# Hybrid RWKV-7 / gated-delta layer on one core: two column blocks of the first projection share one PSUM bank and are taken out by one operation

## The chip, the cores and the metric

The kernel runs on one core of a Trainium2 chip. The metric is device time in microseconds (us). The kernel before takes 1256.82 us as the median of three runs (1255.65 to 1258.12). The profile is one further execution of the same program: 1255.44 us, of which 1253.70 us lie between its first and its last instruction (its span).

The engines are called as in the profile: PE does matmuls (PEld is its weight load), DVE is the vector engine, ACT the scalar engine, POOL the general one, and SP issues most DMAs. Each engine works through its own instructions strictly in the order in which they were laid down when the program was built.

## The reference

One layer with 2048 channels over 256 positions, batch 1, all in float32:

```python
h = rms_norm(x, attn_norm_w)
proj = h @ w_in                                   # 2048 x 6448
y_a = rwkv7_mixer(proj[..., :3360], ...)          # token shift, then a recurrence over 256 steps, 16 heads of 64
y_b = gdn_mixer(proj[..., 3360:], ...)            # conv of width 4 and silu on q, k, v; gated delta rule; gate silu(z)
x = x + concatenate([y_a, y_b]) @ w_out
h = rms_norm(x, ffn_norm_w)
x = x + (silu(h @ w_gate) * (h @ w_up)) @ w_down  # 5632 wide
return rms_norm(x, final_norm_w)
```

Token shift is `p + (prev - p) * mu`, with `prev` the position before. The convolution of the second mixer reads the three positions before as well.

## The kernel before

**Projection.** Positions lie along the free dimension, channels on the 128 partitions. Both operands of every large matmul are split into a high and a low part (`split`, L244): ACT writes the rounded high part `wh`, DVE subtracts it from the source and writes the low part `wl`. One weight tile is 128x1024, loaded by one DMA of SP into `raw` (three buffers), split into `wh` and `wl` (two buffers each) and used by 24 matmuls of 256 columns: 16 of the high part (L220 and L223, in turn) and 8 of the low part (L220). A column block of the first projection has 128 output channels and takes two such tiles, so 48 matmuls, into the first 256 columns of one PSUM bank (tag `pb`, two banks in turn). These projection matmuls are called fillers below, since everything else on PE stands between them.

**Evacuation.** After each block DVE multiplies the bank by `rstd` into an SBUF tile `pr` with four zero columns ahead of it (`evac_norm`, L232; two tiles in turn). Then either the token shift follows (ACT L238, DVE L239), or the convolution (`conv_silu`: ACT L667, three DVE operations at L669), or, for z, nothing but a silu. There are 24 blocks of k, r and v for the first mixer, 16 of q, k and v for the second, and 8 of z. Three blocks at the very start (`ps_first`) go their own way.

**The side work.** The two mixers run beside the projection as generators (`prep`, `chain`, `gdn_v`, `gdn`), which go on as soon as their inputs exist. Each ends in recurrences over four chunks. Ahead of a recurrence stands the inverse of triangular blocks (`tri_inverse`, L336): 62 small DVE operations (L352, L354), a trip through DRAM (`sX`, L360, L363), then two sets of small matmuls (`psF`, `psO`). There are three inverses, one after another in the same buffers: r0 and r1 (first mixer, two halves of its heads) and g (second mixer).

**The second mixer's end.** In its last chunk `psOg` (L938) is scaled by ACT (L942), completed by DVE (L944, eight heads), squared and summed by ACT (L949), turned into a reciprocal root by small DVE operations (L951 and `rsqrt`), applied by ACT (L954), and transposed by PE (`ps_og`, L964). DVE multiplies that with z (L967), and the result is split into `ys`.

**The output projection** (L1015) runs over two halves of its inner dimension: first all 16 blocks with the first mixer's output (16 tiles, 384 fillers), then all 16 with the second mixer's. The second pass can't begin before `ys` of the second mixer is there, and no other work for PE stands between the passes. The feed-forward part follows.

**The order.** Loads, splits and evacuations run at high priority. Which instruction stands where on each engine is laid down by a scheduler that plays the program through when it is built; the side work fills the gaps that it sees. A change of a few instructions can so move others far away.

Of the kernel before, what the change touches and what calls it, by code (L numbers as in the profile page):

```python
# [9 lines left out]
F32 = mybir.dt.float32  # L10
# [3 lines left out]
AF = mybir.ActivationFunctionType  # L14
ALU = mybir.AluOpType
AX = mybir.AxisListType

P = 128
T = 256
# [13 lines left out]
VEC = {}  # L33
# [8 lines left out]
OMU = VEC["om"] - VEC["mu_k"]  # L42
# [7 lines left out]
def trunk_kernel(ctx, tc, xT, vecs, fnw, w_up, a_up, g_up, w_in, w_ab, w_out, w_gu, w_dn, out):  # L50
    nc = tc.nc
    V, S, G, PE, SY = nc.vector, nc.scalar, nc.gpsimd, nc.tensor, nc.sync

    cp_ = ctx.enter_context(tc.tile_pool(name="consts", bufs=1))
    wp = ctx.enter_context(tc.tile_pool(name="weights", bufs=1))
    act = ctx.enter_context(tc.tile_pool(name="act", bufs=4))
    pm = ctx.enter_context(tc.tile_pool(name="pm", bufs=2, space=bass.MemoryType.PSUM))
    dr = ctx.enter_context(tc.tile_pool(name="dr", bufs=1, space=bass.MemoryType.DRAM))

    def hi():  # L60
        return tc.high_priority(offset=HI)
# [11 lines left out]
    def mps(name, tag="mr"):  # L73
        return pm.tile([P, 512], F32, tag=tag, name=name)


    vec = cp_.tile([P, NVEC], F32, name="vec")
# [3 lines left out]
    def vc(name, i=0, rows=slice(0, P)):  # L81
        c = VEC[name] + i
        return vec[rows, c:c + 1]
# [34 lines left out]
    rstd = cp_.tile([P, T], F32, name="rstd")  # L118

    with hi():  # L120
        V.memset(rstd, 0.0)
        ps = mps("ps_warm")
# [6 lines left out]
    GS = cp_.tile([P, T], F32, name="GS")  # L129
    GT = cp_.tile([P, 2, 104], F32, name="GT")  # L130
    egc = cp_.tile([P, 8, NCH], F32, name="egc")
    prs = [cp_.tile([P, 260], F32, name=f"pr{i}") for i in range(2)]
    for pr in prs:
        G.memset(pr[:, 0:4], 0.0)

    def rsqrt(y, xh, tag):

# [27 lines left out]
    def tick():  # L165
        for g in list(side):
            while not g.done and g.step():
                pass
# [8 lines left out]
    def load_split(src, by_k=False, whole=False):  # L177

        with hi():
            if first:  # L180
                raw = first.pop(0)
            else:
                raw = wp.tile([P, 1024], F32, tag="raw", name="raw", bufs=RAW)
                SY.dma_start(out=raw.rearrange("p (c f) -> p c f", c=4) if by_k else raw, in_=src)
            wh = wp.tile([P, 1024], F32R, tag="wh", name="wh", bufs=WH)
            wl = wp.tile([P, 1024], F32R, tag="wl", name="wl", bufs=WL)
            both = [(wh[:, h * 512:h * 512 + 512], wl[:, h * 512:h * 512 + 512]) for h in range(2)]
            if whole:
                split(wh, wl, raw)
                return both  # L190
            it = iter(both)
            return halves_of(raw, lambda: next(it), by_k)

    def halves_of(raw, places, by_k=False):
        parts = []
        r4 = raw.rearrange("p (c k f) -> p k c f", c=4, k=2)
        for h in range(2):
            wh, wl = places()
            src, oh, ol = raw[:, h * 512:h * 512 + 512], wh, wl
            if by_k:  # L200
                src, oh, ol = r4[:, h], wh.rearrange("p (c f) -> p c f", c=4), wl.rearrange("p (c f) -> p c f", c=4)
            S.activation(oh, src, AF.Copy)  # L202
            V.tensor_tensor(ol, src, oh, ALU.subtract)  # L203
            parts.append((wh, wl))
        return parts

    def proj(parts, tag="pb"):

        ps = pm.tile([P, 512], F32, tag=tag, name="psb")
        for j, (src, rhs) in enumerate(parts):  # L210
            products(ps, load_split(src, whole=True), rhs, j == 0, j == len(parts) - 1)
        return ps

    def products(ps, parts, rhs, first, last, by_k=False):

        order = [(k, low) for low in range(2) for k in range(8)]
        for k, low in sorted(order) if by_k else order:
            w = parts[k // 4][low][:, k % 4 * P:k % 4 * P + P]
            rt, ri = rhs[k]
            PE.matmul(ps[:, 0:T], w, rt[:, ri, 0:T], start=(first and k == 0 and not low),  # L220
                      stop=(last and k == 7 and low == 1))
            if not low:
                PE.matmul(ps[:, 0:T], w, rt[:, ri, T:], start=False, stop=False)  # L223
            tick()

    prn = [0]

    def evac_norm(ps):

        prn[0] += 1  # L230
        pr = prs[prn[0] % 2]
        V.tensor_tensor(pr[:, 4:260], ps[:, 0:T], rstd, ALU.mult)  # L232
        return pr

    def evac_shift(ps, mu, out):
        with hi():
            pr = evac_norm(ps)
            S.activation(out, pr[:, 4:260], AF.Copy, scale=vec[:, mu + OMU:mu + OMU + 1])  # L238
            shifted[0] = V.scalar_tensor_tensor(out, pr[:, 3:259], vec[:, mu:mu + 1], out, ALU.mult, ALU.add)  # L239
        return pr  # L240

    shifted = [None]

    def split(hi_ap, lo_ap, src, scale=None):  # L244
        if scale is None:
            S.activation(hi_ap, src, AF.Copy)  # L246
            V.tensor_tensor(lo_ap, src, hi_ap, ALU.subtract)  # L247
        else:
            S.activation(hi_ap, src, AF.Copy, scale=scale)
            V.scalar_tensor_tensor(lo_ap, src, scale, hi_ap, ALU.mult, ALU.subtract)  # L250
# [31 lines left out]
    ps_first = [mps("psb", tg) for tg in ("mc", "mg", "mc")]  # L282
    for q in range(2):
        for i in range(3):
            if not xs:
                split_x(0)
            parts = load_split(w_first[i][q])
            if len(xs) < 4:
                split_x(len(xs))
            products(ps_first[i], parts, [(xs[2 * q + k // 4], k % 4) for k in range(8)], q == 0, q == 1, True)  # L290
# [3 lines left out]
    ps = mps("ps_ss")  # L294
# [11 lines left out]

    xk = [(xs[k // 4], k % 4) for k in range(KB)]

    def proj_in(cb):
        return proj([(w_in[cb, q], xk[8 * q:8 * q + 8]) for q in range(2)])  # L310


    def sigmoid(o, x):
        S.activation(o, x, AF.Tanh, scale=0.5)
# [1 line left out]

    pl = rp.tile([P, 2, T], F32, tag="kt", name="pl", bufs=2)
    for i in range(2):
        evac_shift(ps_first[i], VEC["mu_l"] + i, pl[:, i, :])
    S.activation(twa[0:64, :], pl[0:64, 0, :], AF.Tanh)  # L320
    V.tensor_copy(twa[64:128, :], pl[64:128, 0, :])
    sigmoid(sgd1, pl[:, 1, :])
    pl2 = rp.tile([P, T], F32, tag="al1", name="pl2")
    pr = evac_shift(ps_first[2], VEC["mu_l"] + 2, pl2)
    sigmoid(sgd2[0:32, :], pl2[0:32, :])
    ra, rb = slice(32, 40), slice(64, 72)
# [322 lines left out]
    def rwkv_stream(hf):  # L649
        for gr in range(2):  # L650
            for i, (d, mu, tag, nb) in enumerate(((kt, "mu_k", "kt", 2), (rt, "mu_r", "rt", 2), (vt, "mu_v", "vt", 4))):
                f = hf * 4 + gr * 2
                t = rp.tile([P, 2, T], F32, tag=tag, name=f"{tag}{hf}{gr}", bufs=nb)
                for m in range(2):
                    evac_shift(proj_in(2 + ((hf * 2 + gr) * 3 + i) * 2 + m), VEC[mu] + f + m, t[:, m, :])
                vready[(hf, gr)] = shifted[0]
                d[(hf, gr)] = t


    def conv_silu(ti, b0, outt):  # L660
        for m in range(2):
            ps = proj_in(2 * ti + m)
            tb = outt[:, m, :]
            with hi():
                pr = evac_norm(ps)
                c0 = (b0 + m) * 4
                S.activation(tb, pr[:, 4:260], AF.Copy, scale=vc("conv", c0 + 3))  # L667
                for i in range(3):
                    V.scalar_tensor_tensor(tb, pr[:, 1 + i:257 + i], vc("conv", c0 + i), tb, ALU.mult, ALU.add)  # L669
        with hi():  # L670
            return S.activation(outt, outt, AF.Silu)
# [304 lines left out]
    Side(gdn_v())  # L976
    Side(gdn())
    rwkv_stream(0)
    rwkv_stream(1)
    gdn_stream()  # L980

    for i in range(4):
        z = rp.tile([P, 2, T], F32, tag=("kt", "rt")[i % 2], name="zs", bufs=2)
        if i == 3:

            last2 = [pm.tile([P, 512], F32, tag="pb", name="psb") for _ in range(2)]
            for q in range(2):
                for m in range(2):
                    products(last2[m], load_split(w_in[48 + m, q], whole=True), xk[8 * q:8 * q + 8], q == 0, q == 1)
        for m in range(2):  # L990
            ps = last2[m] if i == 3 else proj_in(42 + 2 * i + m)
            with hi():
                V.tensor_tensor(z[:, m, :], ps[:, 0:T], rstd, ALU.mult)
                if m:
                    S.activation(z, z, AF.Silu)
        zs[i] = z
    drain()
    yg = gout[-1]
# [5 lines left out]
    for src in (yR[0], yR[1], yg[:, 0:4, :], yg[:, 4:8, :]):  # L1004
        t = act.tile([P, 4, 2 * T], F32R, tag="act", name="ys")
# [9 lines left out]
    for q in range(2):  # L1015
        for kb in range(KB):
            ps = proj([(w_out[kb, q], yk[8 * q:8 * q + 8])])
# [4 lines left out]
            if kb % 4 == 0:  # L1022
                pool, tag = ((rp, "ar1"), (rp, "bkn1"), (rp, "UV1"), (act, "act"))[kb // 4]
# [11 lines left out]
    ps = mps("ps_ss2")  # L1035
# [152 lines left out]
    for tb in range(2):  # L1188
        pieces = [(0, 512), (512, 512), (1024, 512)] + [[(1536, 512)], [(1536, 256), (1792, 256)]][tb]
        for j, (c0, w) in enumerate(pieces):  # L1190
            ps = mps("psd", ("mr", "mc", "mg")[nbank[0] % 3])[:, 0:w]
# [101 lines left out]
```

## Time and profile before

| | us |
|---|---|
| median of three runs | 1256.82 |
| the profiled execution | 1255.44 |
| its span | 1253.70 |
| PE busy (8134 matmuls) | 1234.8 (98%) |
| DVE busy (1635 operations) | 834.3 (67%) |
| ACT busy (1199 operations) | 651.3 (52%) |
| mean granted TensorE clock | 0.995 |

Busy time of PE is not all work: matmuls are pipelined, a 256-column one is shown as some 0.28 us long though the next starts 0.12 us after it. So short waits vanish in that row, and long ones show as idle time. The first projection and the side work fill the span up to about 398 us, the first pass of the output projection goes to about 458 us, the second to about 510 us, and the feed-forward part takes the rest. DVE is busiest in the first 350 us.

### The profile page before, as it was taken

The page shows a single profiled execution, that of the slowest core. Times are in us where ns is not written, and L with a number is a line of the kernel's source. Part 1 is how long each engine was busy: PE and PEld are TensorE (multiplying, and loading weights), DVE is VectorE, ACT ScalarE, POOL GpSimd, SP SyncE. Part 2 cuts the span into 40 slices and gives each one's busy share as a digit, 9 for nine tenths or more (in the row PEclk, how much of TensorE's full clock was granted, in tenths as well). Part 3 has the DMA queues.
Part 4 walks back from the last instruction along what each step waited for, and adds up shares of the span by engine and source line. Part 5 has one row for each costly group of instructions (what it writes and reads, how often), then busy time and mean ns, then how long its engine had stood idle before and what let it go on. Part 6 is the DMA issues. An engine that isn't in the chain of part 4 may idle for free.

```text
span 1253.7 us, 21133 instructions
## 1 busy us (share of the span) xinstructions
PE 1234.8 (98%) x8134; PEld 1087.0 (87%) x8134; DVE 834.3 (67%) x1635; ACT 651.3 (52%) x1199; POOL 17.8 (1%) x63
## 2 busy tenths in 40 slices
PE   8999999999999999999999999999999999999997
PEld 8999999999999989888888888888888888878886
DVE  7987887977966877565555555555656565665554
ACT  7575665667546456554444444444444444454443
POOL 3000000000000000000000000000000000000000
PEclk9999999999999999999999999999999999999999
DMA  7455665575573445676666666666676666676641
GB/s 248 153 169 179 169 170 149 169 186 139 196 213 118 145 159 186 172 205 194 190 190 197 188 193 192 194 190 196 187 198 182 189 190 195 203 236 193 193 151 67
DMA packets 175702, 226.68 MB, mean 181 GB/s; under 512 B 52273, under 2 KB 144561, under 8 KB 175345
## 3 DMA queue, kind: packets, MB, share of 16 engines
q1 hardware_dynamic: 170896, 221.54, 60.4%
q10 hardware_dynamic: 4560, 2.74, 0.8%
q8 instruction: 64, 1.05, 0.4%
q0 software_dynamic: 144, 1.05, 0.2%
q14 instruction: 38, 0.30, 0.1%
HBM read 218.75 MB, written 4.46 MB: 178 GB/s over the span
## 4 chain that ended last, share of the span: by engine, by line
PE 88%; DVE 5%; DMA 3%; issue 1%; ACT 1%; SPq 0%; ACTq 0%; DVEq 0%
PE psq L1070 37%; PE psd L1147 17%; PE psb L220 16%; PE psb L223 8%; DVE wl L247 2%; PE psT L1102 1%; DMA sX_r<-X_r 1%; DMA raw_end<-in_w_dn 1%; DMA st_r<-sX_r 1%; PE ps_A L485 1%; PE psd L1198 1%; PE psd L1196 1%; PE psd L1197 1%; DMA A_g<-sG 0%; PE psSg L923 0%
## 5 line engine op out<-in xcount | busy, mean ns | idle before, releaser
L203 DVE TENSOR_TENSOR wl<-raw,wh 128x512 fp32r<-128x512 f32 x524 | 340.7, 692 | 273.5 <-ACT wh L202 271.8
L202 ACT ACTIVATE wh<-raw 128x512 fp32r<-128x512 f32 x524 | 302.5, 626 | 363.9 <-PE psq L1070 192.4
L1070 PE MATMUL psq<-wh,x2s 128*128 128x512 f32 x1408 | 377.4, 390 | 0.8 <-ACT wh L202 0.8
L1070 PEld LDWEIGHTS psq<-wh,x2s 128*128 128x128 f32 x1408 | 263.7, 188 | 56.2 <-ACT wh L202 1.7
L1070 PE MATMUL psq<-wl,x2s 128*128 128x512 f32 x704 | 217.2, 389 | 0.0
L220 PE MATMUL psb<-xs,wh 128*128 128x256 f32 x816 | 206.4, 287 | 2.4 <-ACT wh L202 1.7
L223 PE MATMUL psb<-xs,wh 128*128 128x256 f32 x816 | 206.0, 286 | 0.0
L1147 PE MATMUL psd<-wh,h 128*128 128x512 f32 x640 | 203.2, 391 | 1.0 <-ACT wh L202 1.0
L246 ACT ACTIVATE wh<-raw 128x1024 fp32r<-128x1024 f32 x128 | 135.4, 1058 | 87.4 <-PE psb L223 67.8
L247 DVE TENSOR_TENSOR wl<-raw,wh 128x1024 fp32r<-128x1024 f32 x128 | 156.1, 1220 | 11.1 <-ACT wh L246 10.9
L220 PEld LDWEIGHTS psb<-xs,wh 128*128 128x128 f32 x816 | 156.8, 192 | 4.4 <-ACT wh L202 2.4
L223 PEld LDWEIGHTS psb<-xs,wh 128*128 128x128 f32 x816 | 156.8, 192 | 1.2 <-issue 0.7
L1070 PEld LDWEIGHTS psq<-wl,x2s 128*128 128x128 f32 x704 | 132.0, 188 | 27.6
L1147 PEld LDWEIGHTS psd<-wh,h 128*128 128x128 f32 x640 | 119.2, 188 | 25.8 <-ACT wh L202 1.7
L220 PE MATMUL psb<-xs,wl 128*128 128x256 f32 x816 | 127.1, 287 | 0.9 <-DVE wl L247 0.7
L1147 PE MATMUL psd<-wl,h 128*128 128x512 f32 x320 | 124.6, 389 | 0.0
L220 PEld LDWEIGHTS psb<-xs,wl 128*128 128x128 f32 x816 | 109.8, 192 | 2.8 <-DVE wl L247 1.1
L1147 PEld LDWEIGHTS psd<-wl,h 128*128 128x128 f32 x320 | 60.1, 188 | 12.7
L223 PE MATMUL psb<-ys,wh 128*128 128x256 f32 x256 | 64.6, 288 | 2.5 <-DVE ys L247 2.5
L220 PE MATMUL psb<-ys,wh 128*128 128x256 f32 x256 | 64.8, 289 | 0.2 <-ACT ys L246 0.2
L223 PEld LDWEIGHTS psb<-ys,wh 128*128 128x128 f32 x256 | 50.1, 196 | 2.8 <-DVE ys L247 2.7
L1155 DVE TENSOR_TENSOR acc<-acc,psd 128x512 f32<-128x512 f32 x80 | 49.5, 682 | 1.8 <-PE psd L1147 1.8
(315 smaller groups left out, 1026.8 us busy)
## 6 DMA issues: line engine op xcount, KB each, us to landing
raw<-in_w_gu SPq DMA_DIRECT2D x176, 512.0 KB, 4.9
raw<-in_w_in SPq DMA_DIRECT2D x99, 512.0 KB, 3.5
raw<-in_w_dn SPq DMA_DIRECT2D x80, 512.0 KB, 4.3
raw<-in_w_out SPq DMA_DIRECT2D x32, 512.0 KB, 3.5
raw_end<-in_w_dn SPq DMA_DIRECT2D x8, 512.0 KB, 4.2
xraw<-in_xT SPq DMA_DIRECT2D x8, 256.0 KB, 5.8
x<-in_xT SPq DMA_DIRECT2D x1, 2048.0 KB, 9.7
raw<-in_w_ab SPq DMA_DIRECT2D x2, 512.0 KB, 4.9
```

The lines of the kernel that those rows point to most:

```text
L202: S.activation(oh, src, AF.Copy)
L203: V.tensor_tensor(ol, src, oh, ALU.subtract)
L220: PE.matmul(ps[:, 0:T], w, rt[:, ri, 0:T], start=(first and k == 0 and not low), stop=(last and k == 7 and low == 1))
L223: PE.matmul(ps[:, 0:T], w, rt[:, ri, T:], start=False, stop=False)
L246: S.activation(hi_ap, src, AF.Copy)
L247: V.tensor_tensor(lo_ap, src, hi_ap, ALU.subtract)
L485: PE.matmul(psA[h][:, ch, :], bk[hr, ch].rearrange("p a t -> p (a t)"), ar[hr, p, ch].rearrange("p a t -> p (a t)"), start=True, stop=True)
L1070: last = PE.matmul(banks[tb], t[:, ri, o + tb * P:o + tb * P + P], w, start=(k == 0 and o == 0 and w is wh), stop=(k == KB - 1 and w is wl))
L1102: ms.append(PE.transpose(ps[b][:, o:o + P], sg[tb][:, (2 * b + i) * P:(2 * b + i) * P + P], ident))
L1147: m = PE.matmul(banks[tb * 2 + cg], st, parts[cg][w], start=(i == 0 and w == 0 and st is hh), stop=(i == n - 1 and st is hl))
L1155: V.tensor_tensor(acc[:, tb, cs], acc[:, tb, cs], banks[tb * 2 + cg], ALU.add)
L1196: PE.matmul(ps, hh, wh, start=(i == 0), stop=False)
```

## The change

Two neighbouring column blocks now go to the two halves of one bank, and one DVE operation takes both out. `proj_in2` runs the blocks one after the other, tiles in the same sequence as before. `prs` is one tile with two halves, in place of two tiles in turn. The shift and the convolution still work on one block at a time, but both blocks of a pair now follow the pair's evacuation. Of the 46 blocks that went through `proj_in`, 23 pairs are made; the three first blocks and the last two of z keep an evacuation each.

```diff
-    prs = [cp_.tile([P, 260], F32, name=f"pr{i}") for i in range(2)]
-    for pr in prs:
-        G.memset(pr[:, 0:4], 0.0)
+    prs = cp_.tile([P, 2, 260], F32, name="prs")
+    G.memset(prs[:, :, 0:4], 0.0)
...
+    def proj_in2(cb):
+        ps = pm.tile([P, 512], F32, tag="pb", name="psb")
+        for m in range(2):
+            for q in range(2):
+                products(ps[:, m * T:m * T + T], load_split(w_in[cb + m, q], whole=True), xk[8 * q:8 * q + 8],
+                         q == 0, q == 1)
+        return ps
...
     def evac_norm(ps):
-        prn[0] += 1
-        pr = prs[prn[0] % 2]
-        V.tensor_tensor(pr[:, 4:260], ps[:, 0:T], rstd, ALU.mult)
-        return pr
+        V.tensor_tensor(prs[:, :, 4:260], ps.rearrange("p (m t) -> p m t", m=2), rstd[:, None, :].to_broadcast([P, 2, T]),
+                        ALU.mult)
+
+    def shift(pr, mu, out):
+        S.activation(out, pr[:, 4:260], AF.Copy, scale=vec[:, mu + OMU:mu + OMU + 1])
+        shifted[0] = V.scalar_tensor_tensor(out, pr[:, 3:259], vec[:, mu:mu + 1], out, ALU.mult, ALU.add)
...
-                for m in range(2):
-                    evac_shift(proj_in(2 + ((hf * 2 + gr) * 3 + i) * 2 + m), VEC[mu] + f + m, t[:, m, :])
+                ps = proj_in2(2 + ((hf * 2 + gr) * 3 + i) * 2)
+                with hi():
+                    evac_norm(ps)
+                    for m in range(2):
+                        shift(prs[:, m], VEC[mu] + f + m, t[:, m, :])
...
     def conv_silu(ti, b0, outt):
-        for m in range(2):
-            ps = proj_in(2 * ti + m)
-            tb = outt[:, m, :]
-            with hi():
-                pr = evac_norm(ps)
+        ps = proj_in2(2 * ti)
+        with hi():
+            evac_norm(ps)
+            for m in range(2):
+                tb, pr = outt[:, m, :], prs[:, m]
...
+        if i < 3:
+            ps = proj_in2(42 + 2 * i)
             with hi():
-                V.tensor_tensor(z[:, m, :], ps[:, 0:T], rstd, ALU.mult)
-                if m:
-                    S.activation(z, z, AF.Silu)
+                V.tensor_tensor(z, ps.rearrange("p (m t) -> p m t", m=2), rstd[:, None, :].to_broadcast([P, 2, T]),
+                                ALU.mult)
```

The program built from it stands in another order at many places. Three are shown.

**DVE, the first pair of k** (`kt`; `pr_123`, `pr_124` and `prs` are the evacuated blocks; the small rows belong to the gates of the second mixer). Before, from the shift of the pair's first block to that of its second:

```order
L239 SCALAR_TENSOR_TENSOR kt_457<-pr_123,vec,kt_457 128x256
L678 TENSOR_SCALAR g_e<-gu 8x256
L247 TENSOR_TENSOR wl<-raw,wh 128x1024
L232 TENSOR_TENSOR pr_124<-psb,rstd 128x256
L315 TENSOR_SCALAR sgd_116<-sgd_116 32x256
L679 TENSOR_TENSOR g_e<-g_e,gu 8x256
L247 TENSOR_TENSOR wl<-raw,wh 128x1024
L689 TENSOR_SCALAR gu<-gu 8x256
L239 SCALAR_TENSOR_TENSOR kt_457<-pr_124,vec,kt_457 128x256
```

The same place after the change:

```order
L236 TENSOR_TENSOR prs<-psb,rstd 128x2x256
L255 TENSOR_TENSOR wl<-raw,wh 128x1024
L687 TENSOR_TENSOR g_e<-g_e,gu 8x256
L320 TENSOR_SCALAR sgd_116<-sgd_116 32x256
L241 SCALAR_TENSOR_TENSOR kt_455<-prs,vec,kt_455 128x256 x2
```

Two evacuations of 256 columns have become one of 2x256, and both shifts stand behind it, with the split of a weight tile between.

**SP, the DRAM trip of inverse g** (`sX_g` is the DRAM copy of the inverse, `st_g` and `TTg` are read from it; `raw<-in_w_in` is a weight tile of the first projection, `raw<-in_w_out` one of the output projection). Before:

```order
L360 DMA sX_g<-X_g 1024x1x32 x2
L184 DMA raw<-in_w_in 128x1024
L363 DMA st_g<-sX_g 128x8x32 x2
L875 DMA TTg<-sX_g 32x16x32 x4
L184 DMA raw<-in_w_in 128x1024 x6
L184 DMA raw<-in_w_out 128x1024 x32
```

After the change:

```order
L365 DMA sX_g<-X_g 1024x1x32 x2
L183 DMA raw<-in_w_in 128x1024 x2
L368 DMA st_g<-sX_g 128x8x32 x2
L883 DMA TTg<-sX_g 32x16x32 x4
L183 DMA raw<-in_w_in 128x1024
L183 DMA raw<-in_w_out 128x1024 x32
```

Behind the read of `st_g` six tiles of the first projection were still to be loaded; now it is one. The inverse stands five weight tiles later.

**ACT, the second mixer's end** (`psOg` is its last chunk's output, `junk,rsg` are its squares and their sums, `wh` the split of one weight tile). Before:

```order
L942 ACTIVATE vnknSg<-psOg 64x4x128 x2
L949 ACTIVATE junk,rsg<-vnknSg 128x128 x2
L246 ACTIVATE wh<-raw 128x1024
L949 ACTIVATE junk,rsg<-vnknSg 128x128 x4
L246 ACTIVATE wh<-raw 128x1024
L949 ACTIVATE junk,rsg<-vnknSg 128x128 x2
L246 ACTIVATE wh<-raw 128x1024 x2
L954 ACTIVATE vnknSg<-vnknSg,rsg 128x128 x8
L246 ACTIVATE wh<-raw 128x1024
L246 ACTIVATE ys<-vnknSg 128x2x256 x4
```

After the change:

```order
L950 ACTIVATE vnknSg<-psOg 64x4x128 x2
L957 ACTIVATE junk,rsg<-vnknSg 128x128 x2
L254 ACTIVATE wh<-raw 128x1024
L957 ACTIVATE junk,rsg<-vnknSg 128x128 x6
L962 ACTIVATE vnknSg<-vnknSg,rsg 128x128 x8
L254 ACTIVATE ys<-vnknSg 128x2x256 x4
```

Five tiles were split between `psOg` and the split of `ys`; now it is one. On PE the same shows as a count: from the last `psOg` to `ps_og` there were 118 fillers, and now there are 22, then the first pass of the output projection is at its end. Counted from the start of the program, the last `psOg` has 2714 fillers ahead of it before and 2810 after; `ps_og` has 2832 in both.

More of the change, by code (lines that the diff above doesn't have):

```diff
@@ L224, in products, with evac_shift @@
             tick()
-    prn = [0]
     def evac_norm(ps):
-        prn[0] += 1
-        pr = prs[prn[0] % 2]
-        V.tensor_tensor(pr[:, 4:260], ps[:, 0:T], rstd, ALU.mult)
-        return pr
-    def evac_shift(ps, mu, out):
+        V.tensor_tensor(prs[:, :, 4:260], ps.rearrange("p (m t) -> p m t", m=2), rstd[:, None, :].to_broadcast([P, 2, T]),
[3 more added lines that the diff above has]
+        shifted[0] = V.scalar_tensor_tensor(out, pr[:, 3:259], vec[:, mu:mu + 1], out, ALU.mult, ALU.add)
+    def evac_shift(ps, mu, out, m=0):
         with hi():
-            pr = evac_norm(ps)
-            S.activation(out, pr[:, 4:260], AF.Copy, scale=vec[:, mu + OMU:mu + OMU + 1])
-            shifted[0] = V.scalar_tensor_tensor(out, pr[:, 3:259], vec[:, mu:mu + 1], out, ALU.mult, ALU.add)
+            pr = prs[:, m]
+            V.tensor_tensor(pr[:, 4:260], ps[:, 0:T], rstd, ALU.mult)
+            shift(pr, mu, out)
         return pr
@@ L307, in trunk_kernel @@
     xk = [(xs[k // 4], k % 4) for k in range(KB)]
-    def proj_in(cb):
-        return proj([(w_in[cb, q], xk[8 * q:8 * q + 8]) for q in range(2)])
     def sigmoid(o, x):
@@ L318, in trunk_kernel @@
     for i in range(2):
-        evac_shift(ps_first[i], VEC["mu_l"] + i, pl[:, i, :])
+        evac_shift(ps_first[i], VEC["mu_l"] + i, pl[:, i, :], i)
     S.activation(twa[0:64, :], pl[0:64, 0, :], AF.Tanh)
@@ L660, in conv_silu @@
     def conv_silu(ti, b0, outt):
-        for m in range(2):
-            ps = proj_in(2 * ti + m)
-            tb = outt[:, m, :]
-            with hi():
-                pr = evac_norm(ps)
+        ps = proj_in2(2 * ti)
[3 more added lines that the diff above has]
+                tb, pr = outt[:, m, :], prs[:, m]
                 c0 = (b0 + m) * 4
@@ L989, in trunk_kernel @@
                     products(last2[m], load_split(w_in[48 + m, q], whole=True), xk[8 * q:8 * q + 8], q == 0, q == 1)
-        for m in range(2):
-            ps = last2[m] if i == 3 else proj_in(42 + 2 * i + m)
+        if i < 3:
+            ps = proj_in2(42 + 2 * i)
             with hi():
-                V.tensor_tensor(z[:, m, :], ps[:, 0:T], rstd, ALU.mult)
-                if m:
-                    S.activation(z, z, AF.Silu)
+                V.tensor_tensor(z, ps.rearrange("p (m t) -> p m t", m=2), rstd[:, None, :].to_broadcast([P, 2, T]),
+                                ALU.mult)
+        else:
+            for m in range(2):
+                with hi():
+                    V.tensor_tensor(z[:, m, :], last2[m][:, 0:T], rstd, ALU.mult)
+        with hi():
+            S.activation(z, z, AF.Silu)
         zs[i] = z
```

## The prediction

> **What bounds the kernel now.** I read the busy shares first, then the chain that ended last, the windows of the first projection, PE's waits, and at last the timeline around PE's longest wait there.
>
> ```profile
> PE 1234.8 (98%) x8134; PEld 1087.0 (87%) x8134; DVE 834.3 (67%) x1635; ACT 651.3 (52%) x1199; POOL 17.8 (1%) x63
> PE 88%; DVE 5%; DMA 3%; issue 1%; ACT 1%; SPq 0%; ACTq 0%; DVEq 0%
> 50.00:150.00 100.00, 98.74 (x832) 95.30 (x829) 82.88 (x195) 58.09 (x98) 1.89 (x10) 1.00 0.56 168
> 150.00:350.00 200.00, 197.96 (x2267) 187.99 (x2266) 169.70 (x466) 122.44 (x282) 4.83 (x13) 1.00 0.60 172
> 350.00:457.00 107.00, 107.00 (x996) 101.34 (x996) 76.64 (x166) 58.01 (x111) 0.00 (x0) 1.00 0.50 151
> 457.00:470.00 13.00, 10.26 (x72) 9.82 (x72) 8.26 (x13) 5.78 (x9) 0.69 (x1) 0.87 0.45 162
> PE psb L223 <- DVE ys L247: 2.5, 1, 2.5
> PE psb L220 <- ACT wh L202: 1.7, 1, 1.7
> ```
>
> PE is the bound: 98% of the span, 88% of the chain. The windows (PE is the first figure behind the length, DVE the third) show it within the part that changes: between 50 and 457 us PE is idle for 1.26 + 2.04 + 0 = 3.3 us in all, while DVE is busy for 83 to 85% up to 350 us. The change takes no matmul away. So it can gain little, and the question is whether PE is made to wait anywhere. Its longest wait, 2.5 us for `ys`, is where the second mixer's end feeds the second pass of the output projection. There nothing else is left for PE.
>
> **The change, part by part.**
>
> *The evacuations.*
>
> ```profile
> L232 DVE TENSOR_TENSOR pr<-psb,rstd 128x256 f32<-128x256 f32 x43 | 18.0, 421 | 7.0 <-PE psb L220 6.8
> L488 DVE TENSOR_TENSOR AT<-ps_A,tmask 128x512 f32<-128x512 f32 x16 | 10.4, 688 | 2.2 <-PE ps_A L485 2.2
> L669 DVE SCALAR_TENSOR_TENSOR csv<-pr,vec,csv 128x256 f32<-128x256 f32 x24 | 11.4, 477 | 0.0
> L247 DVE TENSOR_TENSOR wl<-raw,wh 128x1024 fp32r<-128x1024 f32 x128 | 156.1, 1220 | 11.1 <-ACT wh L246 10.9
> ```
>
> A pair cost 2 x 421 = 842 ns on DVE. The new form, 2x256 from PSUM times a repeated operand, isn't in the trace. From below one half bounds it (421 ns), from above two (842 ns); L488 is nearest, 512 from PSUM times a repeated mask, and I take its 688 ns. That saves 154 ns a pair, 23 x 0.154 = 3.5 us of DVE (0 to 9.7 by the bounds). PE hides it: with 3.3 us of idle time in that part it can hand back no more than that, and I count 0. The memset that falls away runs on POOL at the start, beside PE's warm-up: 0.
>
> *What waits longer.* A first half now leaves its bank a block later. One `pb` bank in two still comes free 96 fillers after its pair, 11.6 us at the pace below, against 0.7 us for the evacuation: 0. The shared `prs` has to be read before the next pair is written, also 11.6 us later; the longest reading is a convolution, 6 x 0.477 = 2.9 us on DVE: 0. Behind the evacuation DVE then has 0.688 + 2.9 us before it can split a tile for 1.22 us, 4.8 us in all if nothing lies between. From a pair's end, PE has one tile already split (24 fillers, 2.9 us) and the 16 high ones of the next (1.9 us), also 4.8 us. Where that fails PE waits; in the new order a split mostly stands ahead of the convolution, so I count 0, and up to 0.7 us (one more DVE operation of 512) for each of the 8 convolution pairs, 5.5 us, at the high end.
>
> *What moves.* This is the term that counts. The side work has come later against the fillers, most of all the inverses, through DVE and through two loads in SP's queue ahead of the read of `st_g`. Since the fillers are fixed in number, what comes later takes its cover from the end. The timeline there, before:
>
> ```profile
> 442.03 1.09 PE L938 MATMUL psOg<-vnknSg,gates 64*64 64x128 f32 x16
> 443.05 0.39 PE L220 MATMUL psb<-ys,wh 128*128 128x256 f32 x1
> 443.25 1.21 ACT L942 ACTIVATE vnknSg<-psOg 64x512 f32<-64x512 f32 x2 [1.25 <-PE psOg L938]
> 443.88 2.98 DVE L944 SCALAR_TENSOR_TENSOR vnknSg<-psK,GTn,vnknSg 64x128 f32<-64x128 f32 x8 [0.42 <-ACT vnknSg L942]
> ...
> 444.49 0.31 ACT L949 ACTIVATE junk<-vnknSg 128x128 f32<-128x128 f32 x1
> ...
> 445.38 1.04 ACT L246 ACTIVATE wh<-raw 128x1024 fp32r<-128x1024 f32 x1
> ...
> 446.33 0.29 ACT L949 ACTIVATE junk<-vnknSg 128x128 f32<-128x128 f32 x1
> ...
> 447.62 0.31 ACT L949 ACTIVATE junk<-vnknSg 128x128 f32<-128x128 f32 x1
> ...
> 450.33 0.16 DVE L951 SCALAR_TENSOR_TENSOR rsg<-rsg,nq 128x8 f32<-128x8 f32 x1
> ...
> 451.14 0.17 DVE L143 SCALAR_TENSOR_TENSOR rsg<-rsqrt,rsg 128x8 f32<-128x8 f32 x1
> ...
> 454.63 2.45 ACT L954 ACTIVATE vnknSg<-vnknSg,rsg 128x128 f32<-128x128 f32 x8
> ...
> 457.30 1.91 PE L964 MATMUL ps_og<-ident,vnknSg 128*128 128x128 f32 x16
> 457.94 0.75 DVE L967 SCALAR_TENSOR_TENSOR vnknSg<-ps_og,vec,zs 128x512 f32<-128x512 f32 x1
> ...
> 459.41 0.51 PE L220 MATMUL psb<-ys,wh 128*128 128x256 f32 x2 [0.20 <-ACT ys L246]
> 461.71 2.49 DVE L247 TENSOR_TENSOR ys<-vnknSg,ys 128x512 fp32r<-128x512 f32 x4
> 462.45 0.39 PE L223 MATMUL psb<-ys,wh 128*128 128x256 f32 x1 [2.54 <-DVE ys L247]
> ```
>
> From the last `psOg` to `ps_og` go 15.27 us (442.03 to 457.30), and PE has no gap: its 118 fillers from 443.05 to 457.30 take 14.25 us, 0.121 us each. L954 ends at 457.08, 0.22 us before `ps_og`. So the cover fitted almost exactly. After the change PE has 1.02 us of `psOg` and 22 fillers, 22 x 0.121 = 2.66, together 3.7 us. How long does the work take then? From the rows, counted from the start of `psOg`: L942 at 1.22, L944 at 1.85, the first square at 2.46. Two squares, then one tile's split, put the third at 4.30 (446.33), as before. Six more at 0.43 us (three in 447.62 - 446.33 = 1.29) end at 6.9, with no second split between. L951 then starts at some 7.1; before, it stood behind two splits on DVE. Eleven small operations at 0.2 us (451.14 - 450.33 = 0.81 for four steps) end at 9.3. L954 follows at once, without the two tiles that ACT split ahead of it before: 11.85, and with 0.22 us `ps_og` starts at 12.1. **PE waits 12.1 - 3.7 = 8.4 us.** If the work took its old 15.27 us after all, it would be 11.6 us.
>
> Behind `ps_og` before and after are alike: four multiplications, then the split of `ys`. DVE now takes the first low part after two of the four instead of after all, and without a tile's split between; PE resumes some 2 us earlier, but then waits for the later parts, since the last of them comes at about the same time: 0.
>
> *The clock.* The window's granted clock of 0.87 shows what an idle PE costs:
>
> ```profile
> 463.80:467.30 3.50, 3.50 (x19) 3.50 (x19) 0.40 (x1) 0.00 (x0) 0.69 (x1) 0.52 0.29 101
> 463.99 0.41 PE L223 MATMUL psb<-ys,wh 128*128 128x256 f32 x1
> ...
> 466.98 0.41 PE L223 MATMUL psb<-ys,wh 128*128 128x256 f32 x1
> ```
>
> After the wait of 2.54 us the clock was 0.52 for some 3.4 us, and a filler took (466.98 - 463.99) / 14 = 0.214 us: 16 fillers lost 16 x 0.093 = 1.5 us. A wait of 8.4 us ahead of it should bring at least one more such stretch; I take one, 1.5 us, with 0 and 3.0 as its ends. [...]
>
> **The sum.** 1255.44 (the profiled execution) + 8.4 + 1.5 = 1265.3 us. The profiled execution was 1.38 us below the median of the runs shown, so the median would be 1266.7; I give **1266 us**.
>
> **The rivals.**
>
> *Longer still.* The second mixer's end keeps its 15.27 us (wait 11.6), the clock drops twice more (3.0), or the convolution pairs stall (5.5). Two of the three give 1255.44 + 11.6 + 3.0 = 1270.0 up to 1255.44 + 11.6 + 5.5 = 1272.5. Against it: each split that stretched the work before is gone from ACT's queue but one.
>
> *Not slower, through DVE.* DVE is what paces PE between 50 and 350 us (83 to 85% busy, 5% of the chain), and 3.5 us less of it come back as PE time, 3.3 us at most: 1255.44 - 3.3 = 1252.1. It decides only if `ps_og` isn't waited for, that is, if the work behind `psOg` takes under 3.7 us. Its own operations speak against it: L944, the squares, the small operations and L954 alone are 2.98 + 8 x 0.43 + 2.2 + 2.45 = 11.1 us one after another, some of them side by side.
>
> *No change.* The wait is there, but PE had lost as much before in waits that its busy time hides (a filler is shown as 0.28 us long and starts 0.12 us after the last), and DVE's relief gives them back. It takes some 8 us in 350; the visible waits are 3.3. Time: 1255 to 1258.
>
> **How the numbers follow.** The forecast of 1266 gets 0.71, the longer one 0.16 (half of it above 1272), no change 0.09, the gain through DVE 0.04. The range goes from the wait of 8.4 less all of PE's visible idle time, without loss of clock (1255.44 + 8.4 - 3.3 = 1260.5, and I leave a little below) to 1272: **1259.5 to 1272**, which leaves out some 0.2. A measurement of this kernel can tell about 0.2%, 2.5 us, from no change. Faster by more 0.04, within 0.09, slower 0.87.
>
> **What would show it.** Right: among PE's waits a new one of 8 us or more, `ps_og` for ACT's scaling (L954 before), a second stretch of a lower clock beside it, PE as full as before up to there, and 23 evacuations of 2x256 at some 0.69 us. Wrong: `ps_og` without a wait, or the last `psOg` reached by PE much earlier or later than 11.6 us (96 fillers) after its old place at 442 us; in the latter case the waits lie further up, among the inverses.

## The result, and the profile after

The changed kernel takes 1266.03 us as the median of four runs (1262.95 to 1266.80), the kernel before 1256.24 us (1255.57 to 1258.12). The ratio is 1.0067, with a 95% interval of 1.0049 to 1.0084: slower by 8.4 us by the ratio, by 9.8 us by the two medians. A second set of runs (E9 below) gave 1.0061 (1.0042 to 1.0080). The profiled execution of the changed kernel took 1266.71 us, its span is 1265.00 us and its mean granted clock 0.990 (before 0.995). In E4, E7 and E9 below one execution each took 2046 to 2469 us; it counts in their medians and not in their ratios.

First the busy shares of the changed kernel and its evacuations (the page's costliest groups), then PE's five longest waits: who waits for what, us in all, how often, the longest.

```profile
PE 1238.8 (98%) x8134; PEld 1090.8 (86%) x8134; DVE 834.6 (66%) x1612; ACT 650.8 (51%) x1201; POOL 17.8 (1%) x62
...
L236 DVE TENSOR_TENSOR prs<-psb,rstd 128x512 f32<-128x512 f32 x20 | 13.7, 686 | 4.8 <-PE psb L228 4.7
```

```profile
PE ps_og L972 <- ACT vnknSg L962: 7.7, 1, 7.7
PE psb L228 <- ACT wh L201: 2.7, 1, 2.7
PE psR L570 <- DVE X_g L359: 2.2, 1, 2.2
PE ps_A L490 <- DVE bk L480: 1.4, 1, 1.4
PE ps_warm L123 <- DVE rstd L121: 1.3, 1, 1.3
```

The new wait of 7.7 us at `ps_og` for ACT's scaling is the largest; the 2.5 us for `ys`, PE's longest wait before, is gone from the list (the second row, 2.7 us, belongs to the kernel's start). The joined evacuations take 0.686 us. Two waits in the side work are new or longer, both for DVE and both near the inverses: `psR` 2.2 us (0.5 before) at 331 us and `ps_A` 1.4 us at 199 us.

The same windows as before, first figure PE, third DVE, then the granted clock behind POOL:

```profile
50.00:150.00 100.00, 99.06 (x834) 95.80 (x834) 78.94 (x174) 58.21 (x98) 1.66 (x8) 1.00 0.57 165
150.00:350.00 200.00, 195.70 (x2186) 185.70 (x2187) 165.78 (x431) 118.16 (x259) 4.51 (x14) 0.98 0.57 160
350.00:457.00 107.00, 107.00 (x1028) 101.11 (x1025) 77.98 (x179) 55.96 (x107) 0.53 (x1) 1.00 0.54 172
```

Between 150 and 350 us PE is idle for 4.3 us, before for 2.0, at a clock of 0.98 instead of 1.00. And the timeline of the second mixer's end in the changed kernel (start, us, engine, what, idle time before it and its releaser):

```profile
459.78 1.09 PE L946 MATMUL psOg<-vnknSg,gates 64*64 64x128 f32 x16
...
461.01 1.21 ACT L950 ACTIVATE vnknSg<-psOg 64x512 f32<-64x512 f32 x2 [1.25 <-PE psOg L946]
...
461.63 2.98 DVE L952 SCALAR_TENSOR_TENSOR vnknSg<-psK,GTn,vnknSg 64x128 f32<-64x128 f32 x8 [0.42 <-ACT vnknSg L950]
...
466.66 0.17 DVE L959 SCALAR_TENSOR_TENSOR rsg<-rsg,nq 128x8 f32<-128x8 f32 x1 [0.47 <-ACT junk L957]
...
468.87 2.44 ACT L962 ACTIVATE vnknSg<-vnknSg,rsg 128x128 f32<-128x128 f32 x8 [2.24 <-DVE rsg L142]
471.37 3.68 PE L972 MATMUL ps_og<-ident,vnknSg 128*128 128x128 f32 x16 [7.68 <-ACT vnknSg L962]
...
473.31 0.63 ACT L254 ACTIVATE ys<-vnknSg 128x512 fp32r<-128x512 f32 x1 [1.99 <-DVE vnknSg L975]
474.04 0.68 DVE L255 TENSOR_TENSOR ys<-vnknSg,ys 128x512 fp32r<-128x512 f32 x1
```

Read from marks like these, the loss can be placed. One filler is 0.121 us, and 96 fillers (11.6 us) now stand ahead of the last `psOg` that stood behind it.

| start of, us | before | after | after, less the 96 fillers moved | lost or won up to here |
|---|---|---|---|---|
| last `psOg` | 442.03 | 459.78 | 448.2 | 6.1 lost |
| `ps_og` | 457.30 | 471.37 | | 7.9 more lost |
| first `psq` (feed-forward) | 509.87 | 521.31 | | 2.6 won |
| the span's end | 1253.7 | 1265.0 | | 0.2 won |

The first row rests on single traces, and these scatter. E9 is the changed kernel once more, E6 has its instructions in the same order up to there, and E10 has those of the kernel before. Their last `psOg`, in the order E10, E9, E6:

```profile
444.14 1.09 PE L941 MATMUL psOg<-vnknSg,gates 64*64 64x128 f32 x16
456.16 1.09 PE L946 MATMUL psOg<-vnknSg,gates 64*64 64x128 f32 x16
456.66 1.09 PE L946 MATMUL psOg<-vnknSg,gates 64*64 64x128 f32 x16
```

So the first row is 0.4 to 6.1 us, by which two traces are compared, and 2.8 us between the means (443.1 before, 457.5 after). About 1 us of the 6.1 is lost at the kernel's very start: in that trace the clock is at half for 6.8 us from 8.1 us on, before for 3.4 us from 10.0 us on, and the 51st filler starts at 17.56 us instead of 16.52. In E9 the other rows are alike.

### The profile page after: what moved, and what is told of

Same layout as the page of the kernel before. It is cut to its first block, busy times and chain, and to the rows that moved or that the text cites. A ratio compares the mean times of both kernels' runs of the same rounds, so it can differ in the third digit from the quotient of the medians.

```text
span 1265.0 us, 21106 instructions
## 1 busy us (share of the span) xinstructions
PE 1238.8 (98%) x8134; PEld 1090.8 (86%) x8134; DVE 834.6 (66%) x1612; ACT 650.8 (51%) x1201; POOL 17.8 (1%) x62
## 4 chain that ended last, share of the span: by engine, by line
PE 86%; DVE 7%; DMA 3%; issue 1%; ACT 1%; SPq 1%; DVEq 0%; ACTq 0%
PE psq L1083 36%; PE psd L1160 17%; PE psb L228 16%; PE psb L231 8%; DVE wl L255 2%; DMA raw_end<-in_w_dn 1%; PE psT L1115 1%; PE psd L1211 1%; PE psd L1210 1%; PE psd L1209 1%; PE ps_A L490 1%; DMA sX_r<-X_r 0%; PE psSg L931 0%; PE psR L570 0%; DVE X_r L359 0%
## 5 line engine op out<-in xcount | busy, mean ns | idle before, releaser
L255 DVE TENSOR_TENSOR wl<-raw,wh 128x1024 fp32r<-128x1024 f32 x128 | 156.0, 1219 | 19.9 <-ACT wh L254 18.7
L228 PEld LDWEIGHTS psb<-xs,wh 128*128 128x128 f32 x816 | 158.7, 195 | 4.0 <-ACT wh L201 3.1
L231 PEld LDWEIGHTS psb<-xs,wh 128*128 128x128 f32 x816 | 158.5, 194 | 1.4 <-issue 0.5
L228 PE MATMUL psb<-ys,wh 128*128 128x256 f32 x256 | 63.6, 287 | 0.0
L231 PE MATMUL psb<-ys,wh 128*128 128x256 f32 x256 | 63.0, 284 | 0.0
```

## The experiments

Two theories stood at first. *Place*: the time goes because the side work stands later against the fillers, so that the last chain lies bare, whatever form the evacuation has. *Joined operation*: an operation of 0.69 us in one piece on DVE holds up the side chains, pair by pair. "Filler products" in the expectations are the fillers. What each run shows is listed first. The ratio is to the kernel before on the same chip.

| run | what | median, us | ratio (95%) | wait at `ps_og`, us |
|---|---|---|---|---|
| E1 | pairs in one bank, two operations | 1266.65 | 1.0066 (1.0051 to 1.0080) | 7.7 |
| E2 | nothing joined, buffer by block number | 1262.82 | 1.0039 (1.0026 to 1.0052) | 2.5 |
| E3 | k, r, v pairs joined | 1266.57 | 1.0067 (1.0051 to 1.0083) | 5.1 |
| E4 | convolution pairs joined | 1267.11 | 1.0067 (1.0053 to 1.0081) | 7.9 |
| E5 | convolution and z pairs, old buffer turn | 1259.86 | 1.0012 (1.0001 to 1.0024) | none |
| E6 | changed, last normalisation left out | 1258.21 | 1.0005 (0.9994 to 1.0016) | 0.9 |
| E7 | changed, last scaling divided | 1259.46 | 1.0017 (1.0003 to 1.0031) | 3.0 |
| E8 | all pairs but the first three | 1258.88 | 1.0010 (1.0000 to 1.0020) | 5.1 |
| E9 | changed, again | 1265.01 | 1.0061 (1.0042 to 1.0080) | 7.7 |
| E10 | before, low halves of `ys` used last | 1255.98 | 0.9987 (0.9976 to 0.9999) | none |
| E11 | E8 with E7's and E10's edits | 1257.21 | 0.9998 (0.9985 to 1.0011) | 3.0 |

### E1: the same bank, two operations

```diff
     def evac_norm(ps):
-        V.tensor_tensor(prs[:, :, 4:260], ps.rearrange("p (m t) -> p m t", m=2), rstd[:, None, :].to_broadcast([P, 2, T]),
-                        ALU.mult)
+        for m in range(2):
+            V.tensor_tensor(prs[:, m, 4:260], ps[:, m * T:m * T + T], rstd, ALU.mult)
```

> Both blocks of a pair still go to the halves of one bank, but each half is taken out by an operation of its own, both behind the pair's last product: 46 operations of about 0.42 us instead of 23 of 0.69 us. The schedule puts the side work at the same products as the changed kernel (the last psOg behind 2810 filler products, ps_og behind 2832). Theory P (place: the time is lost because side work is moved later against the projection products, so that the last chain lies bare): a wait of 7 to 9 us at ps_og and 1265 to 1268 us. Rival J (the joined operation itself, 0.69 us in one piece on DVE, holds up the side chains): most of the loss goes, 1256 to 1260 us.

Measured: 1266.65 us, with the waits of the changed kernel:

```profile
PE ps_og L972 <- ACT vnknSg L962: 7.7, 1, 7.7
PE psR L570 <- DVE tmp_g L357: 2.0, 1, 2.0
...
PE ps_A L490 <- DVE bk L480: 1.4, 1, 1.4
```

The joined operation is not what costs. Nor does it bring anything that these runs can tell: DVE is busy for 836.8 us here, for 834.6 us with the joined form, and the ratios are the same. What slows the kernel comes with the pair sharing a bank and being taken out at its end, and the order that follows from it.

### E2 to E4: nothing joined, or some pairs

Edits, from the changed kernel: E3 takes the convolutions and z out block by block again, E4 the k, r and v blocks and z, E2 all of them. For k, r and v that reads

```diff
-                ps = proj_in2(2 + ((hf * 2 + gr) * 3 + i) * 2)
-                with hi():
-                    evac_norm(ps)
-                    for m in range(2):
-                        shift(prs[:, m], VEC[mu] + f + m, t[:, m, :])
+                for m in range(2):
+                    evac_shift(proj_in(2 + ((hf * 2 + gr) * 3 + i) * 2 + m), VEC[mu] + f + m, t[:, m, :], m)
```

> No pair is joined; only the buffer is chosen by the block's number in its pair instead of in turn. The last psOg stands behind 2738 products (before: 2714), so 94 are left for the last chain (before 118, changed kernel 22). Theory P: a wait at ps_og of 0 to 2.9 us (chain 12.1 to 15.3 us less 1.02 us and 94 x 0.121 us), no clock drop among the inverses, 1255 to 1260 us. Rival J: nothing is joined, so as before, 1256 us.

> Only the twelve pairs of the first mixer (k, r, v) are joined. The first inverse of the first mixer stands where the changed kernel has it (behind 1298 products), the last psOg behind 2762, so 70 products are left. Theory P: a wait at ps_og of 2.6 to 5.8 us, the clock drop at the first inverse as in the changed kernel, 1259 to 1264 us. Rival J: 12 of 23 pairs, about half the loss, 1261 us; then the ps_og wait would be no longer than before.

> Only the eight pairs of the second mixer's convolutions are joined. The first mixer's inverses stand as early as before (behind 1199 and 1730 products), the last psOg as late as in the changed kernel (2813, 19 products left). Theory P: a wait at ps_og of 7 to 9 us and none of the new waits and clock drops among the first mixer's inverses, so 1261 to 1265 us. Rival J: 8 of 23 pairs, a third of the loss, 1259 us. Rival F (the first mixer's inverses carry most of the loss): 1256 to 1259 us.

All three came out slower than expected, E2 by 2.8 us beyond its range. The waits at `ps_og` lie where theory *place* puts them (2.5, 5.1 and 7.9 us), so they follow the number of fillers left. But more was lost, and E2 has nothing joined at all. Its longest waits:

```profile
PE ps_og L972 <- ACT vnknSg L962: 2.5, 1, 2.5
PE psb L231 <- ACT wh L201: 2.2, 1, 2.2
PE psb L231 <- DVE prs L249: 2.1, 1, 2.1
PE psF_r L384 <- DVE tn_r L377: 1.9, 1, 1.9
PE psb L234 <- DVE ys L258: 1.4, 1, 1.4
```

The third one, `psb` for DVE's `prs`, is PE waiting for a bank, from 40.2 to 42.3 us. Choosing the buffer by the block's number had put the third of the first blocks and the first k block into the same buffer, and DVE could not take the k block out before the third was shifted. E4 has the same wait (2.1 us). Behind it, from 43.09 us on, E2's fillers start 0.21 us apart instead of 0.12, and from 46.73 us on 0.12 us apart again. So E2 and E4 tested that buffer turn as well as what they were made for, and E4's whole loss can't be put down to the convolution pairs. E3 has no such wait; its losses ahead of `ps_og` are spread over several short ones (`ps_A` 2.1, `psS` 1.4, `ps_kq` 1.0 us), and its mean granted clock is 0.994 (changed kernel 0.990). Its last `psOg` starts at 455.05 us; 48 fillers more stand ahead of it (5.8 us), and 7.2 us are lost on the way.

### E5: joined where nothing moves

The convolution and z pairs stay joined, k, r and v don't, and the first blocks take the buffers in the turn of before. The schedule then leaves the last `psOg` at its old place (118 fillers left).

```diff
-        evac_shift(ps_first[i], VEC["mu_l"] + i, pl[:, i, :], i)
+        evac_shift(ps_first[i], VEC["mu_l"] + i, pl[:, i, :], 1 - i)
...
-    pr = evac_shift(ps_first[2], VEC["mu_l"] + 2, pl2)
+    pr = evac_shift(ps_first[2], VEC["mu_l"] + 2, pl2, 1)
```

> The eight convolution pairs and the three pairs of z are joined (11 of 23), the first mixer's blocks are taken out one by one, and the three first blocks use the two buffers in the same turn as before, so that the first k block finds its buffer free. The schedule then leaves the side work where it was before (last psOg behind 2714 products, 118 left). Theory P (place): no wait at ps_og, no wait at about 40 us, 1254 to 1258 us, as before. Rival J (the joined operation): 11 of 23 pairs, about half the loss, 1260 to 1262 us.

Measured: 1259.86 us, ratio 1.0012. That is outside the range given for *place* by 1.9 us, but most of it is the day's level (before, on the same chip, 1257.95 us), and the interval leaves at most 0.24%. PE's waits are those of before, with 2.0 us at `psS` beside them:

```profile
PE psb L234 <- DVE ys L258: 2.5, 1, 2.5
PE psb L231 <- ACT wh L201: 2.5, 1, 2.5
PE psS L590 <- DVE UV L584: 2.0, 2, 1.8
```

Eleven joined pairs cost some 1.5 us (0.1 to 3.0 by the interval) where the last `psOg` stays, not the half of 8 us that the rival asked for. E4, which joins eight of these eleven and lost 0.67%, lost it with the other buffer turn; apart from that turn it differs from E5 only in the z pairs, which it leaves single. No run parts these two.

### E6 and E7: the last chain made shorter

E6 leaves out the normalisation of the second mixer's last two chunks; E7 divides the eight scalings between ACT and DVE and lets each group of transposes wait for its own two heads.

```diff
 E6
-            if x:
+            if x and cp:
+                scaled = [lastf]
+            elif x:
 E7
-                scaled = [S.activation(vn[:, cp, h, :], vn[:, cp, h, :], AF.Copy, scale=rs[:, h:h + 1])
+                scaled = [S.activation(vn[:, cp, h, :], vn[:, cp, h, :], AF.Copy, scale=rs[:, h:h + 1]) if h % 2 == 0 else
+                          V.tensor_scalar(vn[:, cp, h, :], vn[:, cp, h, :], rs[:, h:h + 1], None, ALU.mult)
                           for h in range(8)]
...
-        together(mt, scaled[-1:])
+        for i, ps in enumerate(pss):
+            together(mt[4 * i:4 * i + 4], scaled[2 * i:2 * i + 2])
```

(`lastf` is the last of the eight DVE operations at L952.)

> The changed kernel without the normalisation of the last two chunks of the second mixer (its squares, its root and its scaling are left out); the order on PE is the same, 22 products from the last psOg to ps_og. Theory P: the last chain ends 6.7 us earlier (last fold to ps_og 464.61 to 471.37 us in the trace), the wait at ps_og falls from 7.7 to about 1 us, the clock stays up there (another 1.5 to 3 us) and up to 2.5 us come back as the wait for ys: 1257 to 1262 us. Rival A (the loss lies ahead, among the inverses, and PE would otherwise wait behind): 1264 to 1267 us.

> The changed kernel with the eight scalings of that chain divided between ACT and DVE, and with each transposed group waiting for its own two heads alone. The last psOg then stands behind 2765 products (67 left instead of 22). Theory P: the chain ends about 1.5 us earlier and has 45 x 0.121 = 5.4 us more cover, so the wait at ps_og is 0 to 2.5 us, and the time 1258 to 1263 us. Rival A: 1265 us or more.

E6: 1258.21 us, level with before; some 7 us of the loss go with 6.7 us of chain. Part of that is clock: its mean granted clock is 0.999, the changed kernel's 0.990. Its order on PE is that of the changed kernel, and its waits among the inverses are still there:

```profile
PE psR L570 <- DVE X_g L359: 2.4, 1, 2.4
PE ps_A L490 <- DVE bk L480: 2.2, 2, 1.4
PE psb L228 <- ACT wh L201: 1.8, 2, 1.7
PE psb L231 <- DVE ys L255: 1.4, 1, 1.4
...
PE ps_og L974 <- DVE vnknSg L952: 0.9, 1, 0.9
```

E7, which computes everything, comes to 1259.46 us, 0.44% below the changed kernel by the two ratios (1.0061 and 1.0017). The wait at `ps_og`, 3.0 us, was longer than the 0 to 2.5 us expected, and the profiled execution (1264.87 us) was one of its slower ones.

### E8: all pairs but the first three

```diff
+                if hf == 0 and gr == 0:
+                    for m in range(2):
+                        evac_shift(proj_in(2 + ((hf * 2 + gr) * 3 + i) * 2 + m), VEC[mu] + f + m, t[:, m, :], m)
+                else:
...
```

and the buffer turn of E5. The first inverse then stands nearly at its old place (1219 fillers ahead of it; before 1223, changed kernel 1298).

> All pairs are joined but the three of the first mixer's first group (20 of 23). The first inverse of the first mixer then stands where it was before (behind 1219 products), the last psOg behind 2757, so 75 products are left. Theory P: a wait at ps_og of 3 to 5.5 us (5.1 with 70 left, 2.5 with 94), no clock drop at the first inverse, 1259 to 1263 us. Rival J: 20 of 23 pairs, nearly the whole loss, 1265 us.

Measured: 1258.88 us, 0.1 us below the range. Twenty of 23 pairs cost 0.10%, all 23 cost 0.61 to 0.67%. The waits:

```profile
PE ps_og L979 <- ACT vnknSg L969: 5.1, 1, 5.1
PE psb L231 <- ACT wh L201: 2.1, 1, 2.1
PE psS L590 <- DVE UV L584: 1.9, 1, 1.9
```

`ps_A` is not among them and `psR` is down to 0.4 us, and the last `psOg` starts at 448.3 us, against 459.8 and 456.2 us in the two traces of the changed kernel. It has 53 fillers fewer ahead of it, 6.4 us; the rest, 5.0 or 1.4 us, the changed kernel loses further up. So the joined operation falls as the cause.

The length of the wait at `ps_og` does not set the time by itself. E3 has the same 5.1 us there and lost 0.67%: its last `psOg` comes 7.2 us late beside the fillers moved, in E8 1.1 us. And E8's 5.1 us show as 0.10% (0.00 to 0.20%, so 2.5 us at most). Some of it comes back behind `ps_og`, where the wait of 2.5 us for `ys` is gone and the trace wins 1.9 us. The rest isn't explained: this trace, the slowest of E8's eleven executions (1260.18 us), ends 4.7 us after that of the kernel before.

### E9: the changed kernel again

> The changed kernel once more, beside the next two on one chip. Theory P: the same waits as in its first trace (7.7 us at ps_og, about 2.2 us before the second half's psR, about 1.5 us behind the first psF_r), 1264 to 1268 us; where the time differs between executions, it differs by half-clock stretches (1.5 us for each 3.41 us), not by the waits.

1265.01 us. The wait at `ps_og` is 7.7 us once more, but my expectation was too simple: the wait at `psR` is 1.1 us instead of 2.2, so waits differ between executions too. The mean granted clock is 0.992 instead of 0.990: 0.97 instead of 0.93 in the first 50 us, and 1.00 instead of 0.97 from 300 to 350 us, where `psR` lies.

### E10 and E11: a faster version

E10 is the kernel before; in the first block of the second pass of the output projection the products with the low half of `ys` come last.

```diff
-            if not low:
+            if not low and not late_lo:
                 PE.matmul(ps[:, 0:T], w, rt[:, ri, T:], start=False, stop=False)
             tick()
+            if low and late_lo:
+                w = parts[k // 4][0][:, k % 4 * P:k % 4 * P + P]
+                PE.matmul(ps[:, 0:T], w, rt[:, ri, T:], start=False, stop=(last and k == 7))
...
-            ps = proj([(w_out[kb, q], yk[8 * q:8 * q + 8])])
+            ps = proj([(w_out[kb, q], yk[8 * q:8 * q + 8])], late_lo=(q == 1 and kb == 0))
```

> The kernel before, in which the first block of the second half of the output projection takes the sixteen products of the high weight half with the high activations and of the low weight half first, and those with the low activation halves (ys, DVE's work) last. Theory W (the 2.5 us wait for ys behind ps_og and the half-clock stretch after it stand alone on the path): the wait falls to under 1 us, 1253 to 1256 us. Rival: the wait turns up at the next product or at a weight load, no change, 1257 to 1258 us.

> Twenty of 23 pairs joined (all but the first mixer's first group), the scalings of the last chain divided between ACT and DVE with each transposed group waiting for its own heads, and the same late low halves. 71 products stand between the last psOg and ps_og. Theory P: the wait at ps_og falls from 5.2 to 0.5 to 2.5 us, 1254 to 1258 us, level with before or a little below. Rival J (20 joined operations cost by themselves): 1260 us or more.

E10 takes 1255.98 us, 2.0 us less than before; the interval (0.9976 to 0.9999) only just excludes 1. The wait for DVE's `ys` is gone, and the mean granted clock is 0.997 (before 0.995). Three short waits for ACT's high half remain, 1.5 us in all where I expected less than 1:

```profile
PE psb L220 <- ACT ys L249: 1.5, 3, 1.2
```

It is the fastest version here, if only just ahead of the kernel before. E11, with twenty pairs joined, is level with before, though it has E10's edit as well; its wait at `ps_og`, 3.0 us, is longer than the 0.5 to 2.5 us expected.

## Why the prediction was right, and where not

**The total and its main term** were right. 1266 us was forecast and 1266.03 measured, and the new wait at `ps_og` was put at 12.1 - 3.7 = 8.4 us: it is 7.7 us. The work from `psOg` to `ps_og` took 11.59 us, not 12.1, and PE's own work under it 3.9 us, not 3.7. Of the 0.5 us, 0.2 lie at the start of the small operations (6.88 us after `psOg`, forecast 7.1), and 0.1 is a slip: 9.3 + 2.45 is 11.75, not 11.85. The two scaled tiles fewer in ACT's queue show in the timeline: the small operations end and the scaling starts at once, 468.87. E6 shows the price of it from the other side: without the last normalisation the wait is 0.9 us and the loss is gone.

**The evacuations**: 0.686 and 0.69 us against 0.688 forecast. No wait for `prs` or for a bank arose in the changed kernel, and the time saved on DVE bought nothing, as counted (E1). The rival of a gain through DVE falls with it.

**"The inverses move, and PE stays full up to there"** was wrong. The sum counted only the end of the fillers: the last `psOg` was to be reached 11.6 us later and was reached 17.75 us later in one trace, 14.1 us in the other, against the kernel before's first trace. `psR` and `ps_A` waited (2.2 and 1.4 us), and a stretch of half clock followed each (3.4 us, from 332.4 and 199.2 us on). The place was named as a sign of error in the prediction, but it had no price there, for I had taken each inverse to find enough other work beside it. All traces together point the same way. I took the start of the last `psOg` in each, less that of the kernel before and less 0.121 us for each filler moved ahead of it. In the six traces whose first inverse stands behind 1298 fillers it is 2.5 to 7.2 us late; in the five where it stands behind 1219 or 1223, -0.1 to 3.1 us (E2 and E4, with their wait for a bank, are left out). The two ranges overlap, for traces of one and the same order differ by 2 to 4 us there. So that the loss goes with the place of the side work is made likely, and its size isn't shown.

**"Behind `ps_og` alike: 0"** was wrong the other way: 2.6 us won. The prediction had PE resume some 2 us earlier and lose that again in waits for the later parts of `ys`; no such wait is on PE's list. Before, the split of a weight tile stood between DVE's multiplications:

```profile
458.61 1.22 DVE L247 TENSOR_TENSOR wl<-raw,wh 128x1024 fp32r<-128x1024 f32 x1
```

So the first low part came after all four, 4.4 us after `ps_og` had started. After the change it comes after two of them, with no tile between, 2.7 us after it (474.04). The 16 transposes meanwhile ran at half clock (3.68 us instead of 1.91). E10 takes the wait of 2.54 us for `ys` away by itself and wins 2.0 us.

**The clock**, +1.5 us, was mis-sized in place and number. In the changed kernel's trace there are 20.5 us at half clock up to 1240 us (from 8.1, 199.2, 332.4 and 468.9 us on), before 6.8. Beside `ps_og` itself it is 3.4 us more, mostly under the wait, and 3.4 us more at the kernel's start; the two stretches at 199 and 332 us, near the inverses, were not foreseen. The 3.0 us at the upper end of this term was an estimate, two stretches like the one before. So the errors nearly cancel: a loss further up that the sum did not have (0.4 to 6.1 us by single traces) against the 1.5 us of clock that it had, and 2.6 us won behind. The sum itself came to 1266.7 us for the median, and the four executions spread from 1262.95 to 1266.80 us. That 1266 was met to 0.1 us is luck; that a new wait of some 8 us at `ps_og` makes the kernel slower is not.

**What stays open**: why traces of one and the same order differ by 2 to 4 us up to the last `psOg`; why E3 loses so much in short waits; and how much of E4's loss is the buffer turn.

## What to carry to other kernels

Handing two results over together at the second one's end delays whatever waited for the first; where a schedule was just covered, price the cover at its end and at the places moved, not the operation saved. A wait that goes can leave the next to come forward, and a wait that comes can swallow one behind it: behind the 7.7 us at `ps_og`, 2.6 us came back. Before a loss is placed by one trace, a second trace of the same order shows how far single traces differ (here 2 to 4 us). And a control that undoes an edit must undo its side edits too: here the order of two buffers cost more than half as much as the change (E2).

## What the runs showed of the chip

PE's granted clock was at half (0.50) in stretches of 3.41 us or twice that. Up to 1240 us they begin, before, at 9.98 and 463.95 us (3.41 us each), and in the changed kernel at 8.12 us (6.83 us), 199.27 and 332.39 us (3.41 us each) and 468.92 us (6.83 us). In each of the two traces the beginnings lie whole multiples of 3.413 us apart, to 0.05 us: 133 of them before, and 56, 39 and 40 in the changed kernel. I cut both traces at such multiples and summed PE's idle time in each piece (full clock, up to 1200 us). Eight pieces have 0.8 us of it or more. Behind six of them, with 1.9 to 3.4 us, the next piece ran at half clock; behind two, with 0.83 us (before, at 457.13 us) and 1.81 us (changed kernel, at 462.09 us), it ran at full clock. Rows of the changed kernel, and three of E6, which has a longer wait at the same `psR` (PE first, the clock behind POOL; the rows of the changed kernel and of before lie within 0.07 us of the cuts):

```profile
195.78:199.20 3.42, 1.48 (x75) 1.16 (x75) 3.07 (x6) 0.21 (x1) 0.00 (x0) 1.00 0.98 238
199.20:202.61 3.41, 3.41 (x25) 3.19 (x22) 3.41 (x8) 1.50 (x3) 0.00 (x0) 0.51 0.83 201
329.00:332.39 3.39, 1.34 (x19) 1.17 (x20) 3.02 (x14) 2.83 (x7) 0.00 (x0) 1.00 0.48 161
332.39:335.80 3.41, 3.41 (x18) 3.41 (x17) 2.27 (x7) 3.23 (x17) 0.00 (x0) 0.50 0.25 54
462.09:465.50 3.41, 1.60 (x14) 1.40 (x12) 3.19 (x9) 3.11 (x13) 0.00 (x0) 1.00 0.47 156
465.50:468.92 3.42, 0.00 (x0) 0.00 (x0) 2.53 (x12) 1.12 (x7) 0.00 (x0) 1.00 0.48 144
468.92:472.33 3.41, 0.96 (x5) 0.96 (x6) 0.00 (x0) 2.40 (x8) 0.00 (x0) 0.50 0.03 10
```

```profile
324.80:328.21 3.41, 1.92 (x17) 1.72 (x15) 3.38 (x10) 0.58 (x1) 0.00 (x0) 1.00 0.39 125
328.21:331.63 3.42, 2.40 (x28) 2.23 (x29) 2.83 (x11) 3.26 (x13) 0.00 (x0) 1.00 0.47 158
331.63:335.04 3.41, 3.30 (x38) 3.03 (x37) 2.53 (x12) 3.29 (x14) 0.00 (x0) 1.00 0.47 154
```

In the changed kernel PE is idle for 1.94 and 2.05 us in the first and the third row, and the clock in the row behind each is 0.51 and 0.50. In E6, with 2.4 us of wait at `psR`, PE is idle for 1.49 and 1.02 us in two rows one after the other, and the clock stays at 1.00. So the length of the wait did not decide it alone. By these rows a wait of 2 us costs 2 us or some 3.5 (an estimate: 1.5 us more for the 16 fillers of one stretch at half clock).

The same rows of the kernel before, at its 16 transposes (1.91 us from 457.30 us on):

```profile
457.07:460.48 3.41, 2.65 (x22) 2.20 (x20) 2.96 (x5) 1.59 (x3) 0.00 (x0) 1.00 0.46 156
460.48:463.90 3.42, 1.45 (x12) 1.45 (x13) 3.42 (x7) 1.90 (x3) 0.00 (x0) 1.00 0.48 153
463.90:467.31 3.41, 3.41 (x19) 3.41 (x18) 0.30 (x1) 0.00 (x0) 0.69 (x1) 0.51 0.31 106
```

In the row of the transposes PE was idle for 0.76 us, and the clock of the next row is 1.00. That next row, idle for 1.97 us with the wait for `ys`, is the one ahead of the half clock at 463.9 us.
